# A last chunk of 2048 output columns: second token half summed whole up to the tail, and only the tail in two pieces

## The chip, the cores and the metric

One core of one Trainium2 chip runs the whole program. The metric is the device time of one execution in microseconds; lower is better. TensorE (PE) multiplies, VectorE (DVE) and ScalarE (ACT) do the elementwise work, GpSimd (POOL) a little of it, and SyncE (SP) issues most transfers. Sums of products are kept in PSUM, eight banks of 512 fp32 values on each of 128 partitions.

## The reference

A decoder trunk of two layers on 256 tokens of width 2048: a Mamba-2 layer, then an attention layer, each followed by a gated MLP. What matters here is that each of the four sub-layers ends in a projection to 2048 columns and a LayerNorm over those columns:

```python
def layer_norm(x, g, b):
    mu = jnp.mean(xf, axis=-1, keepdims=True)
    var = jnp.mean(jnp.square(xf - mu), axis=-1, keepdims=True)
    return ((xf - mu) * lax.rsqrt(var + LN_EPS) * g + b)

for layer in range(DEPTH):
    mix = mamba2_mixer(h, ...) if layer < N_A_LAYERS else moba_cross_attention(h, ...)
    h = layer_norm(DEEPNORM_ALPHA * h + mix, ln_mix_g[layer], ln_mix_b[layer])
    ffn = conv_ffn(h, ...)
    h = layer_norm(DEEPNORM_ALPHA * h + ffn, ln_ffn_g[layer], ln_ffn_b[layer])
```

The projections are `mamba_w_out` (4096 rows), `ffn_w_down` of layer 0 (5632), `attn_w_o` (2048) and `ffn_w_down` of layer 1 (5632).

## The kernel before

All weights are streamed once from HBM, in tiles of 512 KB, in the order in which they are used. `load` (L172) issues the transfer of a tile into one of four raw buffers. `split` (L182) turns it into two tiles of a shorter format: ScalarE rounds (`hi`, L209), DVE subtracts (`lo`, L210), and the next load is issued into the raw buffer that this frees. `splits` (L213) decides at each step how far ahead to split: four tiles, and more where `spare` allows tiles to lie in `hT`, a buffer that is free near the end of a projection. Each product of fp32 operands is made of three: hi x hi, hi x lo and lo x hi.

The unit of work is a step, one weight tile; `products` (L310) writes a step's instructions on TensorE. A `Chunk` is the steps that sum one block of 512 output columns. A projection ahead of a norm is four chunks in mode "X": the tokens are the stationary operand, in two halves of 128, and the weights move past them. `half(i, t, piece)` (L221) does step `i` for token half `t`: two rows of 128 weights, three products each, so six products. Without `piece` they are 512 columns wide and go to the accumulator `ch.part[t]`; with it they are 256 wide and go to `ch.piece[piece]`.

Accumulators are pairs of PSUM banks (`acc_pair`, three pairs in turn) or single banks (`tp_tile`, two in turn, also used for transposes).

The fourth chunk of a projection has a `tail` (4 steps, in the last projection 8) and a `head` (2 steps, whose second halves are put off until the third chunk's sums have been read). In the tail all first halves are done first, then all second halves of piece 0, then all of piece 1, so that the norm of token half 0 runs beside the products of half 1. In the kernel before, *every* second half of such a chunk is summed in two pieces of 256 columns (`second`, L239). The pieces have a pair each, of which the first half of the first bank is used, and in the last projection a `tp_tile` each; the second bank of the chunk's own pair is left unused.

`Norm` (L423) holds a norm: `fetch` the residual, `add` (L448; L451 for a whole half, L454 for a piece) it to a chunk's sum and take statistics, `stats`, then `center` and `scale` on DVE, or `all_off` on ScalarE and POOL. `chain` (L919) sets where each of these is issued: `beyond(i, t, q, f)` means right after `half(i, t, q)` has been written, so the place in program order is the place in each engine's queue. `turn` transposes the result on TensorE (L407) and writes it to `hT` for the next stage, beginning with token half 0 while piece 1 of half 1 is still being summed. The last norm (`n3`, L1148 to L1175) has no next stage: `rest` (L1156) finishes and stores each half, and `gb_psum` copies the factors of the norm to PSUM.

Of the kernel before, what the change touches and what calls it, by code (L numbers as in the profile page):

```python
# [21 lines left out]
OP = mybir.AluOpType  # L22
# [14 lines left out]
ALPHA = 4.0 ** 0.25  # L37
# [3 lines left out]
HC = NC // 2  # L41
# [14 lines left out]
LAST = 8  # L56
# [3 lines left out]
def chunks():  # L60

    z, b, c, dt = 0, 2 * DI, 2 * DI + NG * DS, 2 * DI + 2 * NG * DS

    def some(mode, name, layer, c0, n, nk):
        return [(mode, name, layer, c0 + i * NC, nk, False) for i in range(n)]

    def ffn(layer):
        up = [some(m, "ffn_w_up", layer, c + j * NC, 1, KD)[0] for j in range(DFF // NC)
              for m, c in (("W" if j else "X", 0), ("W", DFF))]
        return up + some("X", "ffn_w_down", layer, 0, 4, KF)  # L70

    out = some("W", "mamba_w_in", 0, b, 2, KD)
    out[0] = out[0][:5] + (True,)
    out += some("H", "mamba_w_in", 0, dt, 1, KD) + some("W", "mamba_w_in", 0, c, 2, KD)
    for g in range(NG):
        out += some("W", "mamba_w_in", 0, DI + g * NC, 1, KD) + some("W", "mamba_w_in", 0, z + g * NC, 1, KD)
    out += some("X", "mamba_w_out", 0, 0, 4, DI // P) + ffn(0)
    out += some("X", "w_kv", None, D, 1, KD) + some("W", "w_kv", None, 0, 4, KD) + some("W", "attn_w_q", 0, 0, 4, KD)
    return out + some("X", "w_kv", None, D + NC, 3, KD) + some("X", "attn_w_o", 0, 0, 4, KD) + ffn(1)
# [12 lines left out]
def yoco_kernel(ctx: ExitStack, tc: tile.TileContext, x, lmg, lmb, lfg, lfb, x_t, columns, w, out):  # L92
    nc = tc.nc
# [10 lines left out]
    def acc_pair():  # L104
        return psum.tile([P, 2, NC], F32, tag="acc", name="acc", bufs=3)

    def tp_tile():
        return psum.tile([P, NC], F32, tag="tp", name="tp", bufs=2)
# [17 lines left out]
    steps, plan = [], chunks()  # L126

    class Chunk:
# [7 lines left out]

        def __init__(self, x, head=0, tail=0):
            self.mode, name, _, _, self.nk, self.both = plan.pop(0)  # L140
            self.x, self.head, self.tail = x, head, tail
            self.cut = cut(self.mode, self.nk, self.both)
            self.n = len(self.cut)
            self.per = self.cut[0][3]
            self.nj = max(self.cut[0][1] // P, 1)
            self.paired = self.mode == "W" and name != "mamba_w_in"
            self.first = len(steps)
            for s in range(self.n):
                steps.append((self, s))
            self.end = len(steps)  # L150
            self.last = self.end - 1
# [69 lines left out]
    def half(i, t, piece=None):  # L221

        ch, s = steps[i]
        h, l = hi_t[i], lo_t[i]
        sl = slice(0, NC) if piece is None else slice(piece * HC, (piece + 1) * HC)
        a = ch.part[t] if piece is None else ch.piece[piece]
        ts = slice(t * P, (t + 1) * P)
        for kk in range(2):
            k = 2 * s + kk
            th = ch.x.hi(k)[:, ts]  # L230
            nc.tensor.matmul(a, th, h[:, kk, sl], start=k == 0, stop=False)  # L231
            nc.tensor.matmul(a, th, l[:, kk, sl], start=False, stop=False)  # L232
        run(inner, (i, t, piece))
        for kk in range(2):
            k = 2 * s + kk
            nc.tensor.matmul(a, ch.x.lo(k)[:, ts], h[:, kk, sl], start=False, stop=k == ch.nk - 1)  # L236
        run(outer, (i, t, piece))

    def second(i):  # L239

        if steps[i][0].tail:
            half(i, 1, 0)
            half(i, 1, 1)
        else:
            half(i, 1)

    def done(i):
        hi_t.pop(i), lo_t.pop(i)
# [61 lines left out]
    def products(i):  # L310
        ch, s = steps[i]
        if ch.mode == "W":
            if s == 0:
                ch.part = []
            if s == 0 or (not ch.both and s == ch.n // 2):
                ch.part += [acc_pair() for _ in range(1 + ch.both)]
        elif s == 0:
            a = acc_pair()
            ch.part = [a[:, 0, :], a[:, 1, :]] if ch.mode == "X" else [a]
            if ch.tail:  # L320
                ch.part.pop()
                ch.piece = [tp_tile()[:, :HC] if ch.tail == LAST else acc_pair()[:, 0, :HC] for _ in range(2)]
        if ch.mode != "X":
            return whole(i)
        half(i, 0)
        if i >= ch.end - ch.tail:
            if i < ch.last:
                return splits(i)
            for q in range(2):
                for j in range(ch.end - ch.tail, ch.end):  # L330
                    half(j, 1, q)
                    if q:
                        done(j)
        elif s < ch.head - 1:
            if ch.tail:
                splits(i)
        elif s == ch.head - 1:
            for j in range(ch.first, i + 1):
                if j < i or ch.tail:
                    splits(i, 1)  # L340
                second(j)
                done(j)
        else:
            run(mid, i)
            splits(i)
            second(i)
            done(i)

    post, pre, mid, inner, outer = {}, {}, {}, {}, {}
# [11 lines left out]
    def amid(i, f, *a):  # L361
        mid.setdefault(i, []).append((f, a))
# [5 lines left out]
    def beyond(i, t, q, f, *a):  # L368

        outer.setdefault((i, t, q), []).append((f, a))  # L370
# [52 lines left out]
    class Norm:  # L423
# [24 lines left out]
        def add(self, c, h, q=None):  # L448
            r = self.r[c][:, h]
            if q is None:  # L450
                nc.vector.scalar_tensor_tensor(r, r, ALPHA, self.chs[c].part[h], op0=OP.mult, op1=OP.add)  # L451
            else:
                v = r[:, q * HC:(q + 1) * HC]
                nc.vector.scalar_tensor_tensor(v, v, ALPHA, self.chs[c].piece[q], op0=OP.mult, op1=OP.add)  # L454
            for w in (0, 1) if q is None else (q,):
                nc.vector.bn_stats(self.st[:, h, 2 * c + w, :], r[:, w * HC:(w + 1) * HC])

        def add2(self, c):
            for h in range(2):
# [459 lines left out]
    def chain(norm, nxt=None, after=None):  # L919

        chs = norm.chs
        last = chs[3].last
        at(chs[0].first, norm.open)
        for c in range(4):
            at(max(chs[0].first, chs[c].last - 7), norm.fetch, c)
            if c < 3:
                at(chs[2].first + 3 + c, norm.fetch_gb, c)
                amid(chs[c].end, norm.add2, c) if c < 2 else beyond(chs[2].end, 0, None, norm.add2, c)
        beyond(last, 0, None, norm.add, 3, 0)
        beyond(last, 0, None, norm.stats, 0)  # L930
        if not nxt:
            return
        beyond(last, 0, None, norm.center, 0, 0)
        beyond(last, 1, 0, norm.scale, 0, 0)
        for e in range(SPARE):
            spare[last - SPARE + 1 + e] = 4 + 4 * e
        n = nxt.first

        def turn(c, h):
            turn_half(norm.r, c, h)  # L940

        beyond(last, 1, 0, norm.all_off, 1, 0)
        beyond(last, 1, 0, norm.add, 3, 1, 0)
        beyond(last - 2, 1, 1, turn, 0, 0)
        beyond(last, 1, 1, norm.add, 3, 1, 1)
        beyond(last, 1, 1, norm.stats, 1)
        beyond(last, 1, 1, norm.center, 0, 1)
        beyond(n, 0, None, norm.scale, 0, 1)
        beyond(n, 0, None, turn, 1, 0)
        beyond(n + 1, 0, None, norm.fetch_gb, 3)  # L950
        beyond(n + 1, 0, None, norm.center, 1, 1)
        beyond(n + 1, 0, None, norm.scale, 1, 1)
        within(n + 2, 0, None, turn, 0, 1)
        beyond(n + 2, 0, None, norm.all_off, 2, 0)
        beyond(n, 1, None, turn, 1, 1)
        beyond(n, 1, None, norm.center, 2, 1)
        beyond(n, 1, None, norm.scale, 2, 1)
        beyond(n + 1, 1, None, norm.all_off, 3, 0)
        beyond(n + 2, 1, None, turn, 2, 0)
        beyond(n + 2, 1, None, norm.center, 3, 1)  # L960
        beyond(n + 3, 0, None, turn, 2, 1)
        beyond(n + 3, 0, None, norm.scale, 3, 1)
        beyond(n + 4, 0, None, turn, 3, 0)
        beyond(n + 4, 1, None, turn, 3, 1)
        for c in range(4):
            at(n + 3 + c, norm.store, c)
        at(n + 6, after)
# [19 lines left out]
    n3 = Norm(down1, keep(2), lfg[1], lfb[1], gb_last, lambda c: tok_view(out[0], c))  # L987
# [142 lines left out]
    for h in range(HEADS):  # L1130
        i, j = divmod(h, 4)
# [16 lines left out]
    end = n_steps - 1  # L1148
# [7 lines left out]
    def rest(h):  # L1156
# [9 lines left out]
        for q in range(2):  # L1166
            n3.norm(3, h, slice(q * HC, (q + 1) * HC))

    beyond(end, 0, None, n3.gb_psum, 3)
    beyond(end, 0, None, rest, 0)  # L1170
    beyond(end, 1, 0, n3.add, 3, 1, 0)
# [47 lines left out]
```

## Time and profile before

| | |
|---|---|
| median of 3 runs | 2513.02 us |
| lowest, highest | 2512.54, 2513.26 us |
| profiled execution, time | 2512.1 us |
| profiled execution, span from first to last instruction | 2509.8 us |
| granted TensorE clock, mean | 0.998 of full |
| DVE, ACT busy | 66%, 54% of the span |
| DMA | 199 GB/s over the span |

The page gives busy times by engine, the chain of work that ended last, and the costliest groups of instructions. The timeline lists instructions by engine in order of time: start in us, duration in us, engine, line, operation, output <- input, shapes, and in brackets the idle time of the engine before it with what ended that idle time. Consecutive equal instructions are merged (x2, x3), and then the duration is that of the group. A TensorE row lasts longer than the distance to the next, since products are pipelined; what a product costs is the distance.

### The profile page before, as it was taken

Reading aid. Unit: us, or ns where it says so; the run is one execution under the profiler, and the core shown is the slowest. Engines: PE = TensorE matmul, PEld = TensorE weight load, DVE = VectorE, ACT = ScalarE, POOL = GpSimd, SP = SyncE. Lnnn points to the kernel's source line nnn. Section 1 sums busy time; section 2 is a strip of 40 time slices with the busy share of each in tenths; the row PEclk is TensorE's granted clock in tenths of the full one; section 3 lists DMA queues with packets and bytes.
Section 4 is the critical chain, followed back from the end, with each engine's and each line's share of the span. In section 5 each row is a group of like instructions: output and inputs, shape, how many; then the busy total and the mean of one; then the engine's idle time right before and its main releaser. Section 6 shows DMA issues by size and latency. Waiting matters only on the chain.

```text
span 2509.8 us, 36085 instructions
## 1 busy us (share of the span) xinstructions
PE 2497.9 (100%) x13983; PEld 2170.8 (86%) x13983; DVE 1657.9 (66%) x2140; ACT 1365.5 (54%) x1790; POOL 76.4 (3%) x96
## 2 busy tenths in 40 slices
PE   9999999999999999999999999999999999999998
PEld 8888888888888888888888888888888888888887
DVE  7878888755676767675445646645767676765445
ACT  6677787643465655554334445543556555554333
POOL 0000000000200000000000200000200000000001
PEclk9999999999999999999999999999999999999999
DMA  7666655666666556656666665456666556566674
GB/s 260 207 189 205 209 191 190 205 210 220 215 203 193 193 193 193 194 185 202 210 229 204 210 193 175 161 176 227 221 192 197 194 191 194 187 200 201 199 228 161
DMA packets 141739, 502.59 MB, mean 200 GB/s; under 512 B 15856, under 2 KB 16368, under 8 KB 141568
## 3 DMA queue, kind: packets, MB, share of 16 engines
q1 hardware_dynamic: 136448, 482.92, 59.3%
q0 software_dynamic: 4832, 16.85, 2.2%
q8 instruction: 109, 1.79, 0.3%
q14 instruction: 62, 0.51, 0.1%
q10 hardware_dynamic: 288, 0.52, 0.1%
HBM read 491.77 MB, written 8.45 MB: 199 GB/s over the span
## 4 chain that ended last, share of the span: by engine, by line
PE 99%; DMA 0%; DVE 0%; SPq 0%; issue 0%; ACT 0%
PE acc L267 41%; PE acc L270 20%; PE acc L231 11%; PE acc L232 11%; PE acc L236 11%; PE acc L805 1%; PE tp L407 0%; PE tp L236 0%; PE tp L232 0%; PE tp L231 0%; DMA raw<-in_w 0%; PE tp L814 0%; PE acc L788 0%; PE tp L1084 0%; PE tp L1118 0%; PE tp L1110 0%
## 5 line engine op out<-in xcount | busy, mean ns | idle before, releaser
L210 DVE TENSOR_TENSOR lo<-raw,hi 128x1024 fp32r<-128x1024 f32 (+1 forms) x869 | 1060.0, 1225 | 722.6 <-ACT hi L209 596.4
L209 ACT CAST hi<-raw 128x1024 fp32r<-128x1024 f32 (+1 forms) x869 | 909.0, 1049 | 826.8 <-PE acc L236 366.6
L267 PE MATMUL acc<-hT,hi 128*128 128x512 f32 x4480 | 1059.0, 391 | 0.4 <-DVE hT L570 0.3
L267 PEld LDWEIGHTS acc<-hT,hi 128*128 128x128 f32 x4480 | 826.9, 188 | 165.0 <-ACT hi L209 0.9
L270 PEld LDWEIGHTS acc<-hT,lo 128*128 128x128 f32 x4480 | 538.6, 188 | 15.6 <-issue 1.2
L270 PE MATMUL acc<-hT,lo 128*128 128x256 f32 x4480 | 544.6, 277 | 0.0
L232 PE MATMUL acc<-lo,gT 128*128 128x512 f32 (+1 forms) x678 | 254.5, 378 | 0.0
L231 PE MATMUL acc<-hi,gT 128*128 128x512 f32 (+1 forms) x678 | 254.1, 377 | 0.0
L236 PE MATMUL acc<-hi,gT 128*128 128x512 f32 (+1 forms) x678 | 200.7, 377 | 0.0
L232 PEld LDWEIGHTS acc<-lo,gT 128*128 128x128 f32 x678 | 127.7, 188 | 23.3
L231 PEld LDWEIGHTS acc<-hi,gT 128*128 128x128 f32 x678 | 127.6, 188 | 23.1
L236 PEld LDWEIGHTS acc<-hi,gT 128*128 128x128 f32 x678 | 124.9, 188 | 23.6
L232 PE MATMUL acc<-lo,yT 128*128 128x512 f32 (+1 forms) x270 | 98.6, 369 | 0.0
L231 PE MATMUL acc<-hi,yT 128*128 128x512 f32 (+1 forms) x270 | 98.5, 369 | 0.0
L231 PE MATMUL acc<-hi,hT 128*128 128x512 f32 x192 | 78.8, 410 | 0.0
L236 PE MATMUL acc<-hi,yT 128*128 128x512 f32 (+1 forms) x270 | 77.7, 369 | 0.0
L232 PE MATMUL acc<-lo,hT 128*128 128x512 f32 x192 | 75.4, 393 | 0.0
L610 DVE TENSOR_TENSOR u<-u,acc 128x512 f32<-128x512 f32 x108 | 73.5, 681 | 2.3 <-ACT u L609 1.4
L637 DVE SCALAR_TENSOR_TENSOR g<-u,cols,g 128x254 f32<-128x254 f32 (+1 forms) x176 | 73.3, 478 | 2.4 <-ACT g L632 2.4
L1034 ACT CAST gT<-v 128x512 fp32r<-128x512 f32 x44 | 27.3, 621 | 84.5 <-DVE v L1033 84.5
L637 DVE SCALAR_TENSOR_TENSOR v<-u,cols,v 128x254 f32<-128x254 f32 (+1 forms) x176 | 73.2, 478 | 0.0
L469 POOL TENSOR_TENSOR rs<-rs,mhalf 128x1 f32<-128x1 f32 x8 | 7.4, 930 | 1982.1 <-DVE nb L470 1982.1
(223 smaller groups left out, 1911.3 us busy)
## 6 DMA issues: line engine op xcount, KB each, us to landing
raw<-in_w SPq DMA_DIRECT2D x880, 512.0 KB, 3.8
mA<-acum_d POOLq DMA_DIRECT2D x16, 512.0 KB, 6.1
hres<-r POOLq DMA_DIRECT2D x12, 512.0 KB, 7.1
r<-hres SPq DMA_DIRECT2D x12, 512.0 KB, 4.6
eA<-acum_d POOLq DMA_DIRECT2D x16, 128.0 KB, 7.5
r<-in_x SPq DMA_DIRECT2D x4, 512.0 KB, 5.8
gb<-in_ln_mix_g SPq DMA_DIRECT2D x8, 256.0 KB, 4.7
gb<-in_ln_mix_b SPq DMA_DIRECT2D x8, 256.0 KB, 4.9
```

The costliest lines, as they stand in the source:

```text
L209: nc.scalar.copy(h[:, sl], t[:, sl])
L210: nc.vector.tensor_sub(l[:, sl], t[:, sl], h[:, sl].bitcast(F32))
L231: nc.tensor.matmul(a, th, h[:, kk, sl], start=k == 0, stop=False)
L232: nc.tensor.matmul(a, th, l[:, kk, sl], start=False, stop=False)
L236: nc.tensor.matmul(a, ch.x.lo(k)[:, ts], h[:, kk, sl], start=False, stop=k == ch.nk - 1)
L267: nc.tensor.matmul(banks[j], w[:, a, b, js], ch.x.both(k), start=begins, stop=ends, skip_group_check=True)
L270: nc.tensor.matmul(banks[j][:, :S], w[:, a, b, js], ch.x.hi(k), start=begins, stop=ends, skip_group_check=True)
L469: nc.gpsimd.tensor_tensor(self.rs[:, h, :], self.rs[:, h, :], mhalf[:, 0, :], op=OP.pow)
L610: nc.vector.tensor_add(dst, dst, p[:, :, :S])
L637: nc.vector.scalar_tensor_tensor(d, u[:, i % 2, :S - k], c1(self.at_w, w[n - 1 - k] + self.ia + i), d, op0=OP.mult, op1=OP.add)
L805: nc.tensor.matmul(ps[64 * q:64 * q + 64, c, j * P:(j + 1) * P], G[g]["xdt"][:, c, h * 64:(h + 1) * 64], G[g]["A", c][:, h, :], start=True ...
L1034: nc.scalar.copy(h, v[:, sl])
```

## The change

Second halves of the fourth chunk are now summed 512 columns wide, in an accumulator of their own (`part[1]`), up to the tail. Only in the tail are they summed in two pieces, whose first product now starts a new sum. A new DVE instruction, `add_most`, adds `part[1]` to the scaled residual, and the pieces are then added to that without the scaling.

`part[1]` lies in the second bank of the pair that holds piece 0; in the last projection, whose pieces are in `tp_tile`s, in the second bank of the chunk's own pair. `add_most` is issued after the first half of the last but one step, and in the last norm after the statistics of token half 0.

```diff
@@ half(i, t, piece)
+        cut = 2 * (ch.n - ch.tail)
+        k0, k1 = (cut, ch.nk) if piece is not None else (0, cut if t else ch.nk)
...
-            nc.tensor.matmul(a, th, h[:, kk, sl], start=k == 0, stop=False)
+            nc.tensor.matmul(a, th, h[:, kk, sl], start=k == k0, stop=False)
...
-            nc.tensor.matmul(a, ch.x.lo(k)[:, ts], h[:, kk, sl], start=False, stop=k == ch.nk - 1)
+            nc.tensor.matmul(a, ch.x.lo(k)[:, ts], h[:, kk, sl], start=False, stop=k == k1 - 1)
-    def second(i):
-        if steps[i][0].tail:
-            half(i, 1, 0)
-            half(i, 1, 1)
-        else:
-            half(i, 1)
@@ products(i)
             if ch.tail:
-                ch.part.pop()
-                ch.piece = [tp_tile()[:, :HC] if ch.tail == LAST else acc_pair()[:, 0, :HC] for _ in range(2)]
+                if ch.tail == LAST:
+                    ch.piece = [tp_tile()[:, :HC] for _ in range(2)]
+                else:
+                    a = [acc_pair() for _ in range(2)]
+                    ch.piece = [p[:, 0, :HC] for p in a]
+                    ch.part[1] = a[0][:, 1, :]
...
-                second(j)
+                half(j, 1)
...
-            second(i)
+            half(i, 1)
@@ Norm.add
-                nc.vector.scalar_tensor_tensor(v, v, ALPHA, self.chs[c].piece[q], op0=OP.mult, op1=OP.add)
+                nc.vector.tensor_add(v, v, self.chs[c].piece[q])
...
+        def add_most(self):
+            r = self.r[3][:, 1]
+            nc.vector.scalar_tensor_tensor(r, r, ALPHA, self.chs[3].part[1], op0=OP.mult, op1=OP.add)
@@ chain
+        if nxt:
+            beyond(last - 1, 0, None, norm.add_most)
         beyond(last, 0, None, norm.add, 3, 0)
         beyond(last, 0, None, norm.stats, 0)
@@ the last norm
+    beyond(end, 0, None, n3.add_most)
     beyond(end, 0, None, n3.gb_psum, 3)
```

## The prediction

> **What bounds the kernel now.** I read the page's first part, then TensorE's waits, then the order of time inside a last chunk.
>
> ```profile
> span 2509.8 us, 36085 instructions
> PE 2497.9 (100%) x13983; PEld 2170.8 (86%) x13983; DVE 1657.9 (66%) x2140; ACT 1365.5 (54%) x1790; POOL 76.4 (3%) x96
> PE 99%; DMA 0%; DVE 0%; SPq 0%; issue 0%; ACT 0%
> ```
>
> TensorE is busy for the whole span and makes up 99% of the chain that ended last. So the time changes by what TensorE's products take, plus any wait put in front of one. A matmul's own duration is no price here, because matmuls overlap: the price is the distance from start to start. In the timeline of TensorE, a last chunk of the first norm (yT) and, below it, ordinary steps of an earlier chunk (gT):
>
> ```profile
> 644.42 0.40 PE L231 MATMUL acc<-hi,yT 128*128 128x512 f32 x1
> ...
> 645.80 0.28 PE L231 MATMUL acc<-hi,yT 128*128 128x256 f32 x1
> 645.92 0.28 PE L232 MATMUL acc<-lo,yT 128*128 128x256 f32 x1
> ...
> 647.24 0.40 PE L231 MATMUL acc<-hi,yT 128*128 128x512 f32 x1
> ```
>
> ```profile
> 1230.94 0.62 PE L236 MATMUL acc<-hi,gT 128*128 128x512 f32 x2
> ...
> 1232.30 0.62 PE L236 MATMUL acc<-hi,gT 128*128 128x512 f32 x2
> ...
> 1233.66 0.62 PE L236 MATMUL acc<-hi,gT 128*128 128x512 f32 x2
> ```
>
> The mixed step takes 647.24 - 644.42 = 2.82 us: 1.38 for the first token half (six products of 512 columns), 1.44 for the second (twelve of 256, 0.12 each). An ordinary step of two 512-column halves takes 1233.66 - 1230.94 = 2.72, 1.36 for each half.
>
> **Removed: the narrow products.** Every step of a last chunk but its tail changes from mixed to ordinary. By the code these are 16 - 4 = 12 steps for chO, 22 - 4 = 18 for down0, 8 - 4 = 4 for chA and 22 - 8 = 14 for down1, 48 in all. At 2.82 - 2.72 = 0.10 us each: 1.2, 1.8, 0.4 and 1.4, together 4.8 us. The bounds: if only the second half changes (1.44 to 1.36), 3.8; if the mixed pitch has another cause than the width, 0. I take 4.8, as the ordinary step is the same six instructions twice. That the pitch holds for down1, whose pieces lie in tp tiles, and that no step there is held by anything but TensorE, the cast rows show, one a step:
>
> ```profile
> 2463.41 1.05 ACT L209 CAST hi<-raw 128x1024 fp32r<-128x1024 f32 x1 [1.77 <-PE tp L236]
> 2466.23 1.05 ACT L209 CAST hi<-raw 128x1024 fp32r<-128x1024 f32 x1 [1.77 <-PE tp L236]
> ```
>
> ScalarE waits 1.77 of 2.82 us there for TensorE to give a buffer back. At 2.72 it would wait 1.67, so loads and casts follow.
>
> The Trainium skill, "TensorE: Matmul & The Clock Gate", section "Back-to-back issue gap", gives a warm gap of N / 2.4 + 2.5 ns, so one product of 512 columns would save one fixed 2.5 ns over two of 256. As an estimate from that page, 288 pairs would give 0.7 us and not 4.8. The rows disagree: 0.24 us for two narrow ones against 0.227 (1.36 / 6) for a wide one is 0.013 a pair, and the rest of the 0.10 is in the neighbouring half.
>
> **Added: one DVE instruction in each of the four norms, and one wait.** `add_most` is a scalar_tensor_tensor of 128x512 out of PSUM, as the add of token half 0 (L451): 0.69 us. The two adds of the pieces become tensor_add, of the same 128x256; L454 now takes 0.41 and I cost the exchange at nothing (a tensor_add is bound by 0.0 and 0.41, and but for the last of all, it has cover). In the first three norms `add_most` stands in DVE's queue behind the last three splits of weights and ahead of the add of half 0; its accumulator was finished before the tail began, and its residual is there, latest in the third norm, where the fetch is issued 12 us ahead and takes 4.6:
>
> ```profile
> 1754.53 0.37 SPq L440 DMA_DIRECT2D r<-hres  x1
> ```
>
> ```profile
> r<-hres SPq DMA_DIRECT2D x12, 512.0 KB, 4.6
> ```
>
> No transfer changes its place: SP's, POOL's and ScalarE's queues keep their order. In those three, `part[1]` is the second bank of the pair in whose first bank piece 0 is summed, and in the built program the first narrow product of the tail waits for `add_most`, though the banks differ. Behind that product waits all of TensorE. So the place to work out is where DVE's splits end against where TensorE gets to piece 0:
>
> ```profile
> 653.70 3.78 DVE L210 TENSOR_TENSOR lo<-raw,hi 128x1024 fp32r<-128x1024 f32 x3 [2.44 <-ACT hi L209]
> 658.54 0.69 DVE L451 SCALAR_TENSOR_TENSOR r<-r,acc 128x512 f32<-128x512 f32 x1 [1.07 <-PE acc L236]
> ...
> 661.80 0.78 DVE L481 SCALAR_TENSOR_TENSOR r<-r,rs,gb 128x512 f32<-128x512 f32 x1 [0.47 <-POOL rs L469]
> 662.50 0.41 DVE L454 SCALAR_TENSOR_TENSOR r<-r,acc 128x256 f32<-128x256 f32 x1
> ...
> 1382.89 1.23 DVE L210 TENSOR_TENSOR lo<-raw,hi 128x1024 fp32r<-128x1024 f32 x1 [0.57 <-ACT hi L209]
> 1385.69 0.69 DVE L451 SCALAR_TENSOR_TENSOR r<-r,acc 128x512 f32<-128x512 f32 x1 [1.57 <-PE acc L236]
> ...
> 1765.60 1.23 DVE L210 TENSOR_TENSOR lo<-raw,hi 128x1024 fp32r<-128x1024 f32 x1 [0.95 <-ACT hi L209]
> 1767.05 0.69 DVE L451 SCALAR_TENSOR_TENSOR r<-r,acc 128x512 f32<-128x512 f32 x1 [0.22 <-PE acc L236]
> ```
>
> ```profile
> 658.34 0.28 PE L231 MATMUL acc<-hi,yT 128*128 128x256 f32 x1
> ...
> 662.65 0.64 PE L407 MATMUL tp<-ident,r 128*128 128x128 f32 x4
> ...
> 1385.49 0.28 PE L231 MATMUL acc<-hi,gT 128*128 128x256 f32 x1
> ...
> 1766.85 0.28 PE L231 MATMUL acc<-hi,aT 128*128 128x256 f32 x1
> ```
>
> DVE is free of splits at 657.48, 1384.12 and 1766.83; piece 0 starts at 658.34, 1385.49 and 1766.85. DVE begins an independent instruction some 0.08 before the former ends (661.80 + 0.78 = 662.58 against 662.50), and TensorE follows DVE within 0.07 (662.58 to 662.65). So TensorE is let go 0.69 - 0.08 + 0.07 = 0.68 after the splits' end: 658.16, 1384.80, 1767.51, all less what the splits themselves come earlier. TensorE now arrives earlier by 1.2, 1.8 and 0.4: 657.14, 1383.69, 1766.45. How far the splits follow, their casts tell:
>
> ```profile
> 638.98 1.05 ACT L209 CAST hi<-raw 128x1024 fp32r<-128x1024 f32 x1 [1.77 <-PE acc L236]
> ...
> 644.62 1.05 ACT L209 CAST hi<-raw 128x1024 fp32r<-128x1024 f32 x1 [1.77 <-PE acc L236]
> ...
> 655.17 1.05 ACT L209 CAST hi<-raw 128x1024 fp32r<-128x1024 f32 x1 [0.23 <-DMA raw<-in_w]
> ...
> 1371.76 1.05 ACT L209 CAST hi<-raw 128x1024 fp32r<-128x1024 f32 x1 [1.77 <-PE acc L236]
> ...
> 1381.80 1.05 ACT L209 CAST hi<-raw 128x1024 fp32r<-128x1024 f32 x1 [0.74 <-DMA raw<-in_w]
> ...
> 1754.50 1.05 ACT L209 CAST hi<-raw 128x1024 fp32r<-128x1024 f32 x1 [3.10 <-PE acc L236]
> ...
> 1764.52 1.05 ACT L209 CAST hi<-raw 128x1024 fp32r<-128x1024 f32 x1 [1.12 <-DMA raw<-in_w]
> ```
>
> Up to 644.62, 1371.76 and 1754.50 the casts are released by TensorE and move with it; after that they run ahead into hT and wait for weights, whose loads go out when an earlier split frees one of four raw buffers. They are thus a chain of fixed length hung on those casts. By then, counting mixed steps of 2.82 back from the tail, TensorE has saved 0.7 to 0.9 (seven to nine steps), 1.5 (fifteen) and 0.08 (one second half).
> - First norm: let go at 658.16 - 0.8 = 657.36 against 657.14: waits 0.2.
> - Second: 1384.80 - 1.5 = 1383.30 against 1383.69: no wait.
> - Third: 1767.51 - 0.08 = 1767.43 against 1766.45: waits 1.0. Only four steps save there and the splits hardly follow; this norm loses 0.6.
>
> The bounds of the wait: with splits that follow in full 0, 0 and 0.66; with splits that don't move at all 1.0, 1.1 and 1.1. I take 1.2 in sum, since the chain ends in transfers but hangs on TensorE.
>
> The norm's own chain (add of half 0, statistics, scaling, then four transposes on TensorE) pays nothing more: the add comes after `add_most` as the product does, so both are late together. Its transposes are close (scale ends 662.58, they start 662.65), but against piece 0 the add starts no later than now (0.20 after it, where TensorE waits at once). The half-1 chain starts from TensorE's last product and moves with it.
>
> **The last norm** has its pieces in tp tiles, so no product waits. There `add_most` stands behind the statistics of half 0:
>
> ```profile
> 2495.36 0.43 DVE L456 BATCH_NORM_STATS2 bnst<-r 128x6 f32<-128x256 f32 x1
> 2499.92 0.42 DVE L454 SCALAR_TENSOR_TENSOR r<-r,tp 128x256 f32<-128x256 f32 x1 [4.14 <-PE tp L236]
> ```
>
> DVE idles 4.14 us after its half-0 work, which takes up the 0.69; without that cover it would be 0.69 on the end. ScalarE's copy of `gb` into the pair of PSUM that the sums leave has to wait for it as well, and behind the copy wait the center of chunk 1 and its store:
>
> ```profile
> 2489.14 1.02 ACT L512 COPY acc<-gb 128x1024 f32<-128x1024 f32 x1 [4.98 <-DVE r L451]
> 2491.43 0.82 ACT L492 ACTIVATE r<-r,nb,rs 128x512 f32<-128x512 f32 x1 [1.28 <-POOL nb L471]
> ...
> 2502.33 0.81 ACT L492 ACTIVATE r<-r,nb,rs 128x512 f32<-128x512 f32 x1 [10.08 <-POOL nb L471]
> ```
>
> The copy moves from 2489.14 to about 2491.1 (the statistics end at 2490.5), the center by 0.7, and ScalarE has ten idle microseconds behind it. Costed at nothing.
>
> **Sum.** -4.8 + 0.2 + 1.0 = -3.6 us. The profiled execution took 2512.1 us (span 2509.8 and 2.3 around it): 2508.5 by that, span 2506.2. The runs' median of 2513.02 lies 0.9 above the profiled one, so I say 2509.4.
>
> **The rivals.**
> - *The splits follow fully, or the wait costs less than I think*: -4.8 + 0.7 = -4.1, or 2508.9; without any wait 2508.2. For it: the loads move with their buffers. Against: 1754.50 hangs on the second half-step of its chunk. Chance 0.14.
> - *The splits stand still*, the transfers setting their pace: -4.8 + 3.2 = -1.6, or 2511.4. For it: `<-DMA` at all three last casts. Against: those loads wait for buffers, not the other way round. Chance 0.14.
> - *Only the narrow half gains*, because a mixed step's first half owes its 1.38 to alternating between two pairs, which stays in three norms: the gain loses 0.02 x 34 = 0.7; 2510.1. Chance 0.10.
> - *The mixed pitch isn't the width's*, and a step stays near 2.82: no gain, and TensorE waits 0.66 at the third norm alone: 2513.7. Against: the ordinary rows. By the formula of the page named above, the gain would be 0.7 as an estimate, and the end about as before. Chance 0.04.
> - *Slower: the wait for `add_most` outgrows the gain.* Steps taken faster ask for weights sooner, and if the last splits end 1.0 us later than now at all three tails, TensorE waits 2.0, 2.1 and 2.1: 6.2 - 4.8 = +1.4, or 2514.4. It decides from 0.53 us later at each, (4.8 - 3.2) / 3. Against: ordinary chunks run at 2.72 with ScalarE waiting for TensorE. Chance 0.04.
>
> **How the numbers follow.** The forecast holds 0.54. 0.2% of 2513.0 is 5.0 us, about what a measurement can tell from no change: faster means below 2508.0, slower above 2518.0. All cases lie within; the quickest is 0.2 us short of the line, and for it and for gains I don't see I leave 0.10 to faster; 0.03 to slower; 0.87 to the same. The range of 2508.0 to 2511.8 holds every case but the last two, with 0.4 above the third's 2511.4 for a chip's own time; about 0.14 is left out.
>
> **What would show it.** In the changed profile: steps of the last chunks 2.72 apart, casts there waiting 1.67; the wait of the first narrow product on DVE's new line, about 0.2, 0 and 1.0 us; DVE's idle time before the add of half 0 gone in norms one and three; 576 fewer narrow products and 288 more wide ones; nothing new after the last product. I am wrong if steps stay at 2.82, or if TensorE waits over 1.2 us at any tail.

## The result, and the profile after

| | before | changed |
|---|---|---|
| median of 20 runs each | 2512.96 us | 2508.82 us |
| lowest, highest | 2512.45, 2513.77 | 2507.90, 2510.27 |
| ratio of the times | | 0.9984 (0.9978 to 0.9990) |
| profiled execution, time and span | 2512.1, 2509.8 | 2509.57, 2507.2 |

The change takes 4.1 us off, 0.16%, less than the 0.2% that the prediction asks for "faster". The forecast was 3.6 us. The page of the changed kernel, first and fourth part:

```profile
span 2507.2 us, 35513 instructions
PE 2494.8 (100%) x13695; PEld 2157.1 (86%) x13695; DVE 1660.5 (66%) x2144; ACT 1364.9 (54%) x1790; POOL 76.4 (3%) x96
PE 99%; DMA 0%; DVE 0%; ACT 0%; issue 0%; SPq 0%
```

TensorE still sets the end; it has 13983 - 13695 = 288 products fewer (576 narrow ones gone, 288 wide ones new), and DVE has its four additions. The same products in both timelines of TensorE show where the 2.6 us between the two spans arose: the first of the first projection, the first tail product of the first and of the last norm, and the last product of all. Before:

```profile
485.25 0.39 PE L231 MATMUL acc<-hi,yT 128*128 128x512 f32 x1
...
654.26 0.39 PE L231 MATMUL acc<-hT,yT 128*128 128x512 f32 x1
...
2482.78 0.39 PE L231 MATMUL acc<-hT,gT 128*128 128x512 f32 x1
...
2499.49 0.40 PE L236 MATMUL tp<-hT,gT 128*128 128x256 f32 x2
```

After:

```profile
486.64 0.39 PE L234 MATMUL acc<-hi,yT 128*128 128x512 f32 x1
...
654.48 0.39 PE L234 MATMUL acc<-hT,yT 128*128 128x512 f32 x1
...
2479.69 0.39 PE L234 MATMUL acc<-hT,gT 128*128 128x512 f32 x1
...
2496.93 0.40 PE L239 MATMUL tp<-hT,gT 128*128 128x256 f32 x2
```

The profiled execution of the changed kernel was late by 1.39 us before it reached the first step that the change touches. By the first tail that has become 0.22 late, a gain of 1.17 where twelve steps at 0.10 promise 1.2. At the last tail it is 3.09 early, and at the last product only 2.56: 0.53 was lost inside the last tail. From 485 on the gain is 2.56 + 1.39 = 3.95 us. The 1.39 arose in stages that both kernels write alike. Over the ten profiles of this document the first projection starts between 485.03 and 486.64, and the first profile of the changed kernel is the latest of them; nothing is put on it.

The tails themselves, on DVE, after (`add_most` is L460, the add of half 0 is L450):

```profile
657.68 0.68 DVE L460 SCALAR_TENSOR_TENSOR r<-r,acc 128x512 f32<-128x512 f32 x1
658.77 0.69 DVE L450 SCALAR_TENSOR_TENSOR r<-r,acc 128x512 f32<-128x512 f32 x1 [0.41 <-PE acc L239]
...
1384.17 0.69 DVE L450 SCALAR_TENSOR_TENSOR r<-r,acc 128x512 f32<-128x512 f32 x1 [1.06 <-PE acc L239]
...
1764.34 0.68 DVE L460 SCALAR_TENSOR_TENSOR r<-r,acc 128x512 f32<-128x512 f32 x1
1765.14 0.69 DVE L450 SCALAR_TENSOR_TENSOR r<-r,acc 128x512 f32<-128x512 f32 x1
```

and on TensorE, after:

```profile
658.11 0.62 PE L239 MATMUL acc<-hT,yT 128*128 128x512 f32 x2
658.57 0.28 PE L234 MATMUL acc<-hi,yT 128*128 128x256 f32 x1
...
1764.49 0.61 PE L239 MATMUL acc<-hT,aT 128*128 128x512 f32 x2
1765.07 0.39 PE L234 MATMUL acc<-hi,aT 128*128 128x256 f32 x1
1765.29 0.28 PE L235 MATMUL acc<-lo,aT 128*128 128x256 f32 x1
```

Read it by the distances. At the first norm piece 0 starts 0.46 after a group of two wide products, which is their own price (2 x 0.227): no wait, and DVE is done with `add_most` 0.21 earlier (657.68 + 0.68 = 658.36). At the second DVE then idles 1.06. At the third, piece 0 starts 0.58 after the pair instead of 0.45, and the next product 0.22 behind it instead of 0.12: TensorE loses 0.23 us, and `add_most` ends at 1765.02, just ahead. The product's own row has no idle time, since the row before it lasts to 1765.10, and so the waits of PE don't list it. The row of the weight load that goes with the product names it:

```profile
1765.07 0.19 PEld L234 LDWEIGHTS acc<-hi,aT 128*128 128x128 f32 x1 [0.39 <-DVE r L460]
```

So a short wait of TensorE is to be looked for in the rows of PEld and in the distances from start to start.

### The profile page after: what moved, and what is told of

Its sections match the earlier page's. It is cut to its first block, busy times and chain, and to the rows that moved or that the text cites. A ratio compares the mean times of both kernels' runs of the same rounds, so it can differ in the third digit from the quotient of the medians.

```text
span 2507.2 us, 35513 instructions
## 1 busy us (share of the span) xinstructions
PE 2494.8 (100%) x13695; PEld 2157.1 (86%) x13695; DVE 1660.5 (66%) x2144; ACT 1364.9 (54%) x1790; POOL 76.4 (3%) x96
## 3 DMA queue, kind: packets, MB, share of 16 engines
q8 instruction: 107, 1.75, 0.3%
## 4 chain that ended last, share of the span: by engine, by line
PE 99%; DMA 0%; DVE 0%; ACT 0%; issue 0%; SPq 0%
PE acc L262 41%; PE acc L265 20%; PE acc L234 11%; PE acc L239 11%; PE acc L235 11%; PE acc L809 1%; PE tp L406 0%; DMA raw<-in_w 0%; PE tp L818 0%; PE acc L792 0%; PE tp L1090 0%; PE tp L1124 0%; PE tp L1116 0%; PE tp L239 0%; PE tp L234 0%; PE tp L235 0%
## 5 line engine op out<-in xcount | busy, mean ns | idle before, releaser
L234 PE MATMUL acc<-hi,gT 128*128 128x512 f32 (+1 forms) x670 | 260.4, 389 | 0.0
L235 PE MATMUL acc<-lo,gT 128*128 128x512 f32 (+1 forms) x670 | 260.2, 389 | 0.0
L239 PE MATMUL acc<-hi,gT 128*128 128x512 f32 (+1 forms) x670 | 205.9, 389 | 0.0
L234 PE MATMUL acc<-hi,yT 128*128 128x512 f32 (+1 forms) x246 | 95.4, 388 | 0.0
L239 PE MATMUL acc<-hi,yT 128*128 128x512 f32 (+1 forms) x246 | 75.3, 388 | 0.0
```

Of the source, the lines that this page charges most:

```text
L234: nc.tensor.matmul(a, th, h[:, kk, sl], start=k == k0, stop=False)
```

## The experiments

Times are medians of 10 or 11 runs. Four kernels (the products' width, the pair of piece 1, `add_most` behind the add, the early fetch) were run on one chip beside 33 runs of the kernel before (2512.56 us), the other four beside 33 more on the same chip (2512.47).

### The changed kernel again

No edit. It gives the second four a neighbour and shows how far the waits vary between executions.

> The changed kernel once more, beside the next three. Theory: 3.6 to 4.7 us below the kernel before, a wait of 0.2 to 1.0 us in all at the third norm's piece 0 or at its transposes, and 0 to 0.7 at the last weight tile of the last tail, both moving from execution to execution with the landing of transfers.

Measured: 2509.28 us, ratio 0.9987 (0.9978 to 0.9996), 3.2 us less than before. The third tail in this execution, on TensorE:

```profile
1763.82 0.61 PE L239 MATMUL acc<-hT,aT 128*128 128x512 f32 x2
1765.32 0.38 PE L234 MATMUL acc<-hi,aT 128*128 128x256 f32 x1 [0.89 <-DVE r L460]
```

Here piece 0 comes 1.50 after the pair, so TensorE waits 1.05 (and some 0.1 on the next product), on the line that was forecast. The same program waited 0.23 in the other profile. At the second tail, too, piece 0 comes 0.07 late here and the next product 0.11 (the weight load waits 0.33 for L460), where the first profile had no wait. Why the third tail differs, ScalarE's casts show, in the first profile of the changed kernel

```profile
1752.90 1.05 ACT L210 CAST hi<-raw 128x1024 fp32r<-128x1024 f32 x1 [3.02 <-PE acc L239]
...
1762.11 1.05 ACT L210 CAST hi<-raw 128x1024 fp32r<-128x1024 f32 x1 [0.39 <-DMA raw<-in_w]
```

and in this one:

```profile
1752.23 1.05 ACT L210 CAST hi<-raw 128x1024 fp32r<-128x1024 f32 x1 [3.02 <-PE acc L239]
...
1762.36 1.05 ACT L210 CAST hi<-raw 128x1024 fp32r<-128x1024 f32 x1 [1.13 <-DMA raw<-in_w]
```

From the cast that TensorE releases to the last cast of the tail it is 9.21 us in the one and 10.13 in the other; before it was 1764.52 - 1754.50 = 10.02. The last cast waits for its weight tile, 0.39 and 1.13. So the end of the splits, which decides the wait, moves by 0.9 with the landing of transfers. The kernel with the early fetch, below, is the changed kernel as far as the third norm, and its profile lies between: 9.78 us from cast to cast, and 0.82 lost by TensorE at piece 0 and the product after it. Three executions of one order thus lost 0.23, 0.82 and 1.16 at the third tail.

### The products' width, and nothing else

Same accumulators, same adds; but the steps ahead of the tail sum the second half by twelve products of 256 columns into the two halves of the one bank.

```diff
@@ half(i, t, piece)
+        parts = (slice(0, HC), slice(HC, NC)) if t and ch.tail and piece is None else (None,)
+        for p in parts:
+            ap, wp = (a, sl) if p is None else (a[:, p], p)
...
-            nc.tensor.matmul(a, th, h[:, kk, sl], start=k == k0, stop=False)
+                nc.tensor.matmul(ap, th, h[:, kk, wp], start=k == k0 and (p is None or p.start == 0), stop=False, ...)
```

> Everything as in the changed kernel, accumulators and adds too, but the second half of a step ahead of the tail is again twelve products of 256 columns, into the two halves of part[1]'s one bank. Theory (the width sets the pitch): steps of 2.82 us, second half 1.44, first half 1.38; 48 x 0.10 = 4.8 us above the changed kernel, less any wait that goes, 2513 to 2513.6. Rival (what was saved is the changing between three accumulators in three pairs): steps stay at 2.72, 2508.8. Rival (only the second half is the width's, the first half's 0.02 the third accumulator's): 2.80, 2512.6.

Measured: 2513.55 us, ratio 1.0005 (0.9996 to 1.0014): the whole gain is gone, 4.2 to 5.1 us by the changed kernel's two comparisons (3.2 and 4.1 below before, this one 1.0 above). Its last chunk on TensorE, with the first product of three halves in turn (the narrow half of one step, the wide half of the next, the narrow half of that):

```profile
640.78 0.28 PE L237 MATMUL acc<-hi,yT 128*128 128x256 f32 x1
...
642.21 0.40 PE L237 MATMUL acc<-hi,yT 128*128 128x512 f32 x1
...
643.60 0.28 PE L237 MATMUL acc<-hi,yT 128*128 128x256 f32 x1
```

A step is 643.60 - 640.78 = 2.82 again: 1.43 for the narrow half and 1.39 for the wide one. The accumulators are the changed kernel's, and only the width is as it was before. So the narrow products set the pitch, and the wide neighbour's extra 0.02 to 0.03 comes with them. Twice as many products are also twice as many weight loads (the page counts one for each product); no run separates the two. For comparison, the casts of the changed kernel's last chunk, 2.72 apart:

```profile
639.72 1.05 ACT L210 CAST hi<-raw 128x1024 fp32r<-128x1024 f32 x1 [1.66 <-PE acc L239]
642.44 1.05 ACT L210 CAST hi<-raw 128x1024 fp32r<-128x1024 f32 x1 [1.67 <-PE acc L239]
```

### `part[1]` in the pair of piece 1

```diff
-                    ch.part[1] = a[0][:, 1, :]
+                    ch.part[1] = a[1][:, 1, :]
```

Then piece 0 has no wait for `add_most`, while DVE's queue is the same.

> part[1] lies in the second bank of piece 1's pair, so that piece 0's first product no longer waits for add_most and piece 1's, 2.9 us later, does. Theory (the wait is real, and short where the splits follow): no wait of TensorE at any tail's piece 0, piece 0 starting within 0.02 us of the product pitch; the third norm gets back the 0.25 us that its trace showed; time 0.1 to 0.5 us below the changed kernel's 2508.8. Rival (the wait of 1.0 us forecast at the third norm is there in most executions, and that one trace was lucky): 0.8 to 1.2 us below. Rival (nothing waits for add_most): the same time, and the third norm's gap stays.

Measured: 2508.69 us, ratio 0.9985 (0.9976 to 0.9994), as the changed kernel (0.9984), where 0.1 to 0.5 us less was expected. The third tail on DVE and on TensorE:

```profile
1764.19 0.68 DVE L460 SCALAR_TENSOR_TENSOR r<-r,acc 128x512 f32<-128x512 f32 x1
1764.79 0.68 DVE L450 SCALAR_TENSOR_TENSOR r<-r,acc 128x512 f32<-128x512 f32 x1
...
1768.02 0.78 DVE L485 SCALAR_TENSOR_TENSOR r<-r,rs,gb 128x512 f32<-128x512 f32 x1 [0.46 <-POOL rs L473]
```

```profile
1763.93 0.28 PE L234 MATMUL acc<-hi,aT 128*128 128x256 f32 x1
...
1768.01 0.40 PE L239 MATMUL acc<-hT,aT 128*128 128x256 f32 x2
1768.90 0.63 PE L406 MATMUL tp<-ident,r 128*128 128x128 f32 x4 [0.49 <-issue]
```

Piece 0 no longer waits; it starts ahead of `add_most`. But the add of half 0 starts 0.86 after piece 0, where 0.20 was the distance before, and the norm's chain ends later by that much: the transposes start 0.89 after the last pair of narrow products, 0.65 more than the pair's price (2 x 0.12). The row says "issue", but the scaling that they read (L485) ends at 1768.80, 0.10 ahead of them. TensorE pays at the transposes what it did not pay at piece 0. The last split ends at 1764.28, so without `add_most` (0.60 from its start to the add's) the add would have come some 0.06 late. The DVE work ahead of the add is the cost; which instruction meets it is only a matter of banks.

This profile also lost 0.77 us in the last tail, where the first profile of the changed kernel lost 0.53, and again at the split of a late weight tile:

```profile
2484.05 0.50 PE L235 MATMUL acc<-hT,gT 128*128 128x512 f32 x1 [0.46 <-DVE hT L211]
```

So the median alone doesn't show that the transposes took back the gain; the rows of the third tail do.

### `add_most` behind the add of half 0

```diff
-        if nxt:
-            beyond(last - 1, 0, None, norm.add_most)
         beyond(last, 0, None, norm.add, 3, 0)
+        if nxt:
+            beyond(last, 0, None, norm.add_most)
```

This makes piece 0 wait for the whole of half 0's add and statistics, in three norms.

> add_most is issued after the add and the two statistics of half 0 instead of ahead of them, in the first three norms. Theory (all of TensorE stands behind piece 0's first product until add_most ends): the add starts 0.20 us after piece 0 could, then 0.7 + 0.8 + 0.7 us of DVE and 0.07: TensorE waits 2.3 to 2.5 us at each of three tails, some 7 us in all, 2515 to 2516. Rival (the dependency costs nothing, as the banks differ): TensorE goes on at once, only half 0's chain is 0.7 us later and its transposes wait up to 0.7 at each: 2509 to 2511.

Measured: 2516.97 us, ratio 1.0019 (1.0010 to 1.0028), 4.4 above before. TensorE at the first tail:

```profile
656.65 0.61 PE L239 MATMUL acc<-hT,yT 128*128 128x512 f32 x2
659.42 0.39 PE L234 MATMUL acc<-hi,yT 128*128 128x256 f32 x1 [2.15 <-DVE r L460]
```

659.42 - 656.65 - 0.45 = 2.32, with the next product's 0.11 a loss of 2.43, and so at all three tails. Nothing else ties piece 0 to L460 but the shared pair, which the kernel allots as one tile, so the built program's wait between the two banks is real and worth what DVE makes it worth. Three gaps are 7.3 us; the time is 7.6 to 8.5 above the changed kernel's, though that already holds 0.2 to 1.1 of such a wait. The remainder shows in the view by windows (columns: stretch, its length, TensorE, weight loads, DVE, ScalarE and GpSimd busy, granted clock, DMA share, GB/s):

```profile
660.00:663.30 3.30, 3.30 (x18) 3.30 (x17) 1.33 (x2) 0.81 (x1) 2.29 (x3) 0.50 0.00 0
...
1389.00:1393.00 4.00, 4.00 (x36) 4.00 (x34) 2.46 (x6) 0.82 (x1) 2.70 (x4) 1.00 0.15 60
1772.50:1776.50 4.00, 4.00 (x23) 4.00 (x23) 1.28 (x2) 0.81 (x1) 2.92 (x4) 0.57 0.22 87
```

After the first and the third gap the granted clock is near half; after the second it is 1.00. No expectation held that. From the first tail product to the transposes the three tails take 12.30, 10.80 and 12.30 us, where each took 8.4 before: 3.9, 2.4 and 3.9 more. Beyond the gap of 2.43 the half clock thus cost some 1.5 us at each of two tails, and the time came out above the expected 2515 to 2516.

### `add_most` in two instructions

```diff
-            nc.vector.scalar_tensor_tensor(r, r, ALPHA, self.chs[3].part[1], op0=OP.mult, op1=OP.add)
+            nc.vector.tensor_scalar(r, r, ALPHA, None, op0=OP.mult)
+            nc.vector.tensor_add(r, r, self.chs[3].part[1])
```

> add_most is done by two DVE instructions, a scaling of the residual (0.3 to 0.7 us) and a tensor_add out of PSUM (0.7). Theory (DVE's time ahead of the add counts where the splits end late, and is hidden where they end early): the third norm's wait grows by the whole of the new instruction, the first norm's by 0 to 0.4, the second's and the last's by nothing; 0.4 to 1.0 us above the changed kernel. Rival (three tails pay alike): three times the new instruction, 1 to 2 us above. Rival (DVE is beside the path everywhere): the same time.

Measured: 2510.14 us, ratio 0.9990 (0.9982 to 0.9999), 0.86 above the changed kernel in the same batch. DVE and TensorE at the third tail:

```profile
1764.11 0.42 DVE L460 TENSOR_SCALAR r<-r 128x512 f32<-128x512 f32 x1
1764.63 0.69 DVE L461 TENSOR_TENSOR r<-r,acc 128x512 f32<-128x512 f32 x1
```

```profile
1763.41 0.61 PE L239 MATMUL acc<-hT,aT 128*128 128x512 f32 x2
1765.38 0.39 PE L234 MATMUL acc<-hi,aT 128*128 128x256 f32 x1 [1.35 <-DVE r L461]
```

The extra 0.42 lands on TensorE: piece 0 comes 1.97 after the pair, a wait of 1.52 against 1.05 in the changed kernel's profile of this batch. The first two tails wait 0.16 and 0.20, where that profile has 0 and 0.07; the second was expected to stay as it was. With the product after piece 0 the three tails lose 0.85 more. From the first projection to the last product the two profiled executions take 2011.69 and 2010.71 us, 0.98 apart, which fits. The distributions of the times overlap (2508.11 to 2511.71 against 2508.44 to 2509.90), so the medians alone would not carry it; the waits do.

### The last residual fetched six steps earlier

```diff
-            at(max(chs[0].first, chs[c].last - 7), norm.fetch, c)
+            at(max(chs[0].first, chs[c].last - (7 if nxt or c < 3 else 13)), norm.fetch, c)
```

This tests a wait that the prediction did not have. In the changed kernel's first profile the last weight tile comes late in the last norm, on ScalarE, DVE and TensorE:

```profile
2482.03 1.05 ACT L210 CAST hT<-raw 128x1024 fp32r<-128x1024 f32 x1 [2.53 <-DMA raw<-in_w]
```

```profile
2483.12 1.23 DVE L211 TENSOR_TENSOR hT<-raw,hT 128x1024 fp32r<-128x1024 f32 x1 [2.35 <-ACT hT L210]
```

```profile
2483.77 0.39 PE L234 MATMUL acc<-hT,gT 128*128 128x512 f32 x1
2484.40 0.50 PE L235 MATMUL acc<-hT,gT 128*128 128x512 f32 x1 [0.24 <-DVE hT L211]
```

The split ends at 2484.35, and the product that needs it starts 0.63 after the one ahead instead of 0.23: 0.4 of the 0.53 lost in this tail. The residual's transfer, issued at 2477.17, shares that stretch with the weights.

> The last norm fetches its fourth residual at the thirteenth step from the end instead of the seventh. Theory (TensorE's new wait of 0.5 us in the last tail, for the split of the last weight tile, comes from that tile's transfer running beside the fetches, and TensorE now arrives 1.4 us earlier): the last tile lands 1 us or more earlier after its issue (5.2 us in the changed kernel's trace), no wait in the last tail, 0.3 to 0.5 us below the changed kernel. Rival (that landing was an accident of one execution): time the same within 0.2 us.

Measured: 2509.03 us, ratio 0.9986 (0.9977 to 0.9995), and not the 0.3 to 0.5 less than the changed kernel that was expected. Its profile has no such wait; but the changed kernel's second profile has none either, without the edit. Of the six profiles with wide products and the fetch in its old place, two have the wait (0.53 and 0.77); of the two with the early fetch, none. The time is as that of the kernel with the other pair in the same batch (2508.69). Whether the fetch matters stays open: the wait comes and goes by itself.

### `add_most` behind the scaling of half 0, its sum in the chunk's own pair

The experiments above say what a better place needs: not ahead of half 0's add (the cost in DVE's queue), and not in a pair that piece 0 is summed in (the wait). The second bank of the chunk's own pair is free, and DVE has room once half 0 is scaled.

```diff
-                    ch.part[1] = a[0][:, 1, :]
...
-        if nxt:
-            beyond(last - 1, 0, None, norm.add_most)
...
+        beyond(last, 1, 0, norm.add_most)
         beyond(last, 1, 0, norm.add, 3, 1, 0)
```

> part[1] stays in the second bank of the chunk's own pair in all four norms, and in the first three add_most is issued behind the scaling of half 0, just ahead of the add of piece 0. Theory (what costs is DVE's 0.69 us ahead of the add of half 0, be it paid by piece 0 or by the transposes, not the wait as such): no wait at any piece 0, the third norm's transposes late by at most 0.1 us, DVE takes add_most in the idle time ahead of the transposes' second pass; 0.2 to 0.8 us below the changed kernel. Rival (the add of piece 0 and the end of the norm become late instead): a wait of up to 0.7 us moves to the next stage's first steps at each of three norms, 0 to 2 us above.

Measured: 2508.03 us, ratio 0.9981 (0.9973 to 0.9990): 4.4 less than before, and 1.25 less than the changed kernel in the same batch, where 0.2 to 0.8 was expected. Of its eleven runs eight lie at or below 2508.07; the changed kernel's lowest there is 2508.44. Against the changed kernel's first comparison (4.1 less than before) only 0.3 is left, so the size of the gain is known no better than 0.3 to 1.25. DVE at the third tail:

```profile
1764.04 0.68 DVE L449 SCALAR_TENSOR_TENSOR r<-r,acc 128x512 f32<-128x512 f32 x1
...
1767.28 0.77 DVE L484 SCALAR_TENSOR_TENSOR r<-r,rs,gb 128x512 f32<-128x512 f32 x1 [0.46 <-POOL rs L472]
1767.98 0.68 DVE L459 SCALAR_TENSOR_TENSOR r<-r,acc 128x512 f32<-128x512 f32 x1
1768.76 0.42 DVE L452 TENSOR_TENSOR r<-r,acc 128x256 f32<-128x256 f32 x1
```

The add of half 0 (L449) goes first, and `add_most` (L459) stands behind the scaling, where only the add of piece 0 (L452) waits for it. On TensorE no product waits in this tail; the add of half 0 still comes 0.48 after piece 0 started, behind the last split, and the transposes 0.29 late, more than the 0.1 expected. That is what remains of the cost here.

The same with the earlier fetch on top (the edits of this and of the experiment before it):

> The former and the early fetch of the last residual together. Theory (both waits are real and independent): no wait over 0.1 us in any of the four tails, 4.6 to 4.9 us below the kernel before, the whole of 48 x 0.10, and so below the changed kernel by 0.3 to 1.2. Rival (the last tail's wait comes and goes whatever the fetch does): as the former kernel within 0.2 us.

Measured: 2508.19 us, ratio 0.9983 (0.9975 to 0.9992): no difference from the kernel without the fetch, as its rival had it, and less than the 4.6 to 4.9 below before of its theory. In its profile nothing waits in any of the four tails, and from the first projection to the last product it takes 4.61 us less than before. These two have the lowest medians of the versions tried, but their intervals overlap with the changed kernel's.

## Why the prediction was right, point by point

- **The narrow products, -4.8.** Right in size and cause. The casts of the last chunks come 2.72 apart and wait 1.66 to 1.67, as forecast; the first tail's twelve steps gained 1.17 of 1.2. Taken apart from the tails, the four projections gained 1.17, 1.75, 0.39 and 1.41 in the first profile (from the first projection or the transposes ahead to the first tail product), 4.7 together for 1.2, 1.8, 0.4 and 1.4; and where no tail has a wait, in the last kernel tried, the whole gain is 4.61. With narrow products and everything else as in the changed kernel the step is 2.82 and the gain gone. That ends two rivals: *only the narrow half gains* (the halves alternate between two pairs in the changed kernel too, and its step is 2.72; the wide half's 1.39 came back with narrow neighbours alone) and *the mixed pitch isn't the width's*. The 0.7 us that the prediction set beside its sum was no fair rival: in the Trainium skill, "TensorE: Matmul & The Clock Gate", section "Back-to-back issue gap", that formula stands for a product by itself, and the section says that a stream of weight loads and products keeps other distances.
- **Piece 0 waits for `add_most`, 0.2, 0 and 1.0.** The mechanism is right: the wait is named by the profile, grows to 2.43 when `add_most` is put later and by DVE's 0.42 when it is made longer. The sizes were 0, 0 and 0.23 in one profile, 0, 0.18 and 1.16 in another, each with the product after piece 0. The sign that DVE's idle time ahead of the add would go came at the third norm only: at the first it was still 0.41 and 0.61. The step that was mis-sized is "They are thus a chain of fixed length hung on those casts": its length was 10.02 before, and 9.21 and 10.13 after, since its last link is a transfer. Where it was 10.13, the forecast of 1.0 held; the first profile was the kind that the first rival described. To have the typical wait at 1.0 was partly luck: over three executions of this order it was 0.23, 0.82 and 1.16. The forecast should have given that term a spread of one microsecond from execution to execution, not one value.
- **"The norm's own chain … pays nothing more".** Right for the changed kernel, but its reason was half of the matter. With the wait taken away, the chain paid 0.65 at the transposes. The prediction saw that they are close and took the product's wait for the thing to cost; the thing to cost is DVE's queue ahead of the add of half 0, the end of the splits and `add_most` together, and the wait and the late transposes are two ways of paying it.
- **The last norm, nothing; "nothing new after the last product".** Nothing came after the last product, but 0.53 came ahead of it, in one profile of the changed kernel, and 0.77 in that of the kernel with the other pair, for a weight tile that landed late. The prediction costed the order of DVE and ScalarE there and no transfer. No run ties this wait to the change.
- **`add` as `tensor_add`, nothing.** In the row of L452 above it takes 0.42, for the 0.41 of the instruction it replaces.
- **The sum.** -4.8 + 0.23 + 0.53 is -4.0 for the first profile, where the timeline gives -3.95 from the first projection on; -4.8 + 0.18 + 1.16 is -3.5 for the second, where it gives -3.53. The two comparisons measured -4.1 and -3.2, on either side of -3.6. The removed term was known well; that the whole came so near was partly luck, since in the first profile the waits for `add_most` were 1.0 less than forecast and a loss of 0.5 that no term held stood against that.
- **The slower rival.** It needed splits that end later than before at each tail. The experiment with `add_most` late shows that waits at the three tails can outgrow the gain (4.4 us slower than before), but those came of another order, and in part of the clock. The rival's own cause did not come: in the changed kernel's two profiles the first tail lost nothing and the second at most 0.18.

## What to carry to other kernels

Price matmuls by the distance from start to start, and compare whole steps: a narrow half made its wide neighbour dearer too. An instruction added to an engine that is only two thirds busy can still cost TensorE its full length (DVE's 0.42 more became 0.47 of wait), if it stands ahead of the one that a tight chain begins with; look for the gap in that engine's queue and put it there, with an accumulator that no next product shares a tile with. Where a wait hangs on the landing of a transfer, forecast a spread, and settle it with more than one profile.

## What the runs showed of the hardware that was not expected

- **A gap of 2.4 us can cost the clock.** In the kernel with `add_most` late, TensorE lost 2.4 us three times (idle for 2.15 by its row). After two of them the granted clock was 0.50 over 3.3 us and 0.57 over 4.0 (half clock for 3.4 of them); after the other it was 1.00. After the wait of 1.52 us with `add_most` in two instructions the clock from 1765 to 1770 is 1.00. At half clock the narrow products come 0.21 apart instead of 0.12:

```profile
660.48 0.41 PE L234 MATMUL acc<-hT,yT 128*128 128x256 f32 x1
660.69 0.41 PE L235 MATMUL acc<-hT,yT 128*128 128x256 f32 x1
```

  In the changed kernel, without the gap, the clock over the same stretch is 1.00.

  The Trainium skill, "TensorE: Matmul & The Clock Gate", section "Part 1: The HAM clock gate (the "warmup" mystery)", says that the clock falls to half after at least one idle window of about 3.4 us, that it comes back after a busy one of that length, and that the windows run freely. Half clock for 3.3 to 3.4 us agrees with the second; that a gap has to fill a window does not, since a gap of 2.4 us was enough twice in three times. That it depends on where in a window the gap falls would fit, and was not tried.
- **The same program differs by a microsecond in places.** Besides the casts above, the first projection starts up to 1.6 us later in one profile than in another, after stages that are the same in all the kernels.
